# The low part of the attention query as a full 128-row tile

## The chip, the cores and the metric

One core of a Trainium2 chip runs the kernel. The metric is device microseconds (us) of one execution; lower is better. A change of about 0.5% is the least that a measurement of this kernel can tell from no change.

The core has five engines with a queue each: TensorE (PE in the profile; its weight loads are listed apart as PEld), VectorE (DVE), ScalarE (ACT), GpSimd (POOL) and SyncE (SP, which here issues the DMAs). A matrix product on TensorE is two instructions: a weight load of a stationary tile (here up to 128 rows by 128 columns) and a matmul that streams the columns of a moving tile through it. The rows are the partitions over which the product sums.

## The reference

The program is a stack of layers over 512 tokens of width 1024 (and 256 context tokens in the first ones): a recurrent mixer with a scan, then three attention layers. The change is in the attention layers alone. What they compute, cut to what matters:

```python
def block(q_blk):                                     # second layer: differential attention
    s = einsum("bqhcd,bkhcd->bchqk", q_blk, k_all) * scale      # 8 heads x 2 maps of 64 features
    p = softmax(s, axis=-1)
    attn = p[:, 0] - lam * p[:, 1]
    return einsum("bhqk,bkhe->bqhe", attn, v_all)               # 512 queries, 768 keys
...
s = einsum('bhqd,bhkd->bhqk', q, k) * dh ** -0.5      # third and fourth layer: 16 heads of 64 features,
p = softmax(where(mask, s, -inf), axis=-1)            # causal, dilated and memory heads, 512 queries
o = einsum('bhqk,bhkd->bhqd', p, v)
```

All inputs and outputs are float32.

## The kernel before

The first half of the program (`scan`, L935) is the recurrent mixer; it ends at about 1125 us of the execution. `dense` (L1788) does the rest: an output projection with a norm (`out_layer`, L1176), the differential attention (`phase_4`, L1480), an output projection, and twice an attention layer (`phase_5`, L1639) with an output projection behind it.

**Precision.** A float32 operand is split in two parts of the type fp32r, hi + lo = x, and a product is made of hi·hi, hi·lo and lo·hi. Projections do this in three matmuls (`mm3`, L1065; the matmul is at L1070). The scores q·k do it in two, since a head has only 64 features and the array has 128 rows: `split_k` (L1315) stores the keys of an even head as [hi; lo] over the 128 partitions and those of an odd head as [lo; hi]. `split_q` (L1322) stores the queries as [hi; hi] in a tile `q_hi` (L1326 and L1327, ScalarE) and their low part once in a tile `q_lo` (L1328, VectorE): even heads on partitions 0 to 63, odd heads on 64 to 127. `qk_tiles` (L1309) makes these tiles for two pairs of heads, two buffers each: `q_hi` is [128, 4, 512], `q_lo` is [128, 2, 512].

`scores` (L1362) then issues, for one head, one block of 128 queries and up to 512 keys, two products into the same PSUM columns:

```python
P.matmul(ps, q[0][:, 2 * j + h, c], k[h][:, j, a:a + n], start=True, stop=False)   # L1366, 128 rows
P.matmul(ps, q[1][r, j, c], k[h][r, j, a:a + n], start=False, stop=stop)           # L1367, 64 rows
```

The first sums q_hi·(k_hi + k_lo) over 128 rows, the second q_lo·k_hi over the 64 rows `r` of the head.

**Order of the work.** Each attention layer has four steps, one for each two pairs of heads. In a step, `attention` makes eight blocks, each in three pieces: a (scores, maximum, exponential, normalisation), b (transposes of the probabilities, L1566 or L1736) and c (the product with the values, L1577 or L1750). `pipeline` (L1395) runs a two blocks ahead of b and c. In between, `run_streams` (L1074) emits pieces of `side`: the gates of this step and the projections of the keys, queries and values of the next one (`heads`, L1254, `values`, L1299), which are L1070 products. The last step of a layer has only the gates and loads of the output projection beside it. `qk_tiles` of a step is called in the side stream of the step before (`kqv`, L1503; `qkv`, L1664), for the first step ahead of it (`mem`, L1654). The final order on each engine is set by a planner (L1917, `schedule_with_timeline_sim=True`) that works on its own estimates.

Of the other engines' work in a block: VectorE takes the maximum (L1542, L1705), ScalarE the exponential (L1546, L1713, L1717) and a scaling (L1555, L1724), GpSimd the difference of the two maps (L1556) or the scaling of one head (L1726). GpSimd also multiplies with the rope tables (L1293) and splits some of the weights (L1051).

Two other tiles share the names `q_lo` and `q_hi` and so their buffers: the residual of the context (L1796) and that of x (`resid`, L1391). A product over the transposed probabilities at L1750 uses 128 rows by 64 columns of the array, and the transposes and the products with values at L1566, L1577, L1736 all 128 by 128.

Of the kernel before, what the change touches and what calls it, by code (L numbers as in the profile page):

```python
# [8 lines left out]
FT = mybir.dt.float32  # L9
# [57 lines left out]
def rsqrt_dve(E, pool, v, n):  # L67
    """1 / sqrt(v) by Newton steps from a guess out of v's bits."""
    nc = E.nc
    y = pool.tile([128, n], FT, name="rq_y", bufs=2)  # L70
    t = pool.tile([128, n], FT, name="rq_t", bufs=2)
    nc.vector.tensor_scalar(y.bitcast(I32), v.bitcast(I32), -0.5, float(0x5F3759DF), OP.mult, OP.add)
    for _ in range(4):
        nc.vector.tensor_tensor(t, y, y, OP.mult)
        nc.vector.scalar_tensor_tensor(t, t, -0.5, v, OP.mult, OP.mult)
        nc.vector.scalar_tensor_tensor(y, t, 1.5, y, OP.add, OP.mult)
    return y


def ada_columns(E, pool, pp, w, n):  # L80
    """silu(c) @ w for the columns w(kb) = [128, 128 n] of each block kb, as [128, n, 2] in PSUM"""
    nc = E.nc
    ps = pp()
    for kb in range(8):
        nc.tensor.matmul(ps[0:2, 0:128 * n], E.cs[:, kb, :], w(kb), start=(kb == 0), stop=(kb == 7))
    row = pool.tile([2, 128 * n], FT, name="ada_r", bufs=1)
    nc.scalar.copy(row, ps[0:2, 0:128 * n])
    ps = pp()[:, 0:2 * n].rearrange("p (m c) -> p m c", c=2)
    for m in range(n):
        nc.tensor.transpose(ps[:, m, :], row[:, m * 128:(m + 1) * 128], E.ident[0:2, 0:2])  # L90
    return ps


def ada_bias(E, l, m0, n, ps):
    """columns m0 to m0 + n of the modulation of layer l out of those of silu(c) @ ada_w[l]"""
    E.nc.vector.tensor_tensor(E.mod[l][:, m0:m0 + n, :], ps, E.adab[:, l, m0:m0 + n].unsqueeze(2).to_broadcast([128, n, 2]),
                              OP.add)
# [8 lines left out]
def startup(E, hh, hl):  # L106
    """hh, hl: the first layer's normed and modulated [x of the context, x], transposed and split."""
# [59 lines left out]
class Blocks:  # L167
    """[128, 8, 128] of weights at a time in the order of their use, loaded and split ahead of it."""
# [37 lines left out]
class Scan:  # L206
    """The first mixer: its projections, the scan over both directions and its readout, eight pairs of heads in turn.
    Everything of a pair of heads has the heads in the halves of the partitions."""
# [9 lines left out]
    # the projections  # L218
# [10 lines left out]
    def project(self, rhs, evict, last=False):  # L229
        """evict(ps, a, n) for the columns a to a + n of the next block's rows over the tokens; last: uses the second  # L230
        part of the tokens ahead of all else"""
        E = self.E
        ws = self.W.get()
        ps = [self.pj() for _ in rhs]
        n = [0] * len(rhs)
        passes = [(half, part) for part in (((1,), (0, 2)) if last else ((0, 1, 2),)) for half in range(2)]
        for half, part in passes:
            wh, wl = ws[half]
            for gi, (hh, hl, a) in enumerate(rhs):
                terms = [((wh, hh), (wh, hl), (wl, hh))[i] for i in part]  # L240
                for kb in range(4 * half, 4 * half + 4):
                    for w, h in terms:
                        n[gi] += 1
                        E.nc.tensor.matmul(ps[gi][:, :256], w[:, kb % 4, :], h[:, kb, :], start=(n[gi] == 1),  # L244
                                           stop=(n[gi] == 24))
                if n[gi] == 24:
                    evict(ps[gi][:, :256], a, 256)
                yield 0
            if 0 in part:
                self.W.ahead(half)  # L250

    def head_rsqrt(self, x, n, scale, eps, use):
        """use(ps, a, n): ps the broadcast rsqrt(scale * sum of x^2 over each head + eps) of columns a to a + n"""
# [100 lines left out]
    def memory(self):  # L354
        """the memory's keys (normed, transposed) and values of both layers"""
# [41 lines left out]
    def memory_norm(self):  # L397
        """the memory, normed and transposed, to E.MT"""
# [19 lines left out]
    def ada(self, pieces, pool, psum, bufs=2):  # L418
        """more columns of the modulation: the first layer's gates and the second layer's columns"""
# [11 lines left out]
    # the scan  # L431
# [68 lines left out]
    def prep(self, p, g, j, d):  # L500
        """one direction of one head pair over one group of four chunks"""
# [5 lines left out]
        q = d * 64  # L507
# [85 lines left out]
    def fetch(self, k, jds):  # L593
        """the matrices of four chunks that were made ahead of the scan"""
# [23 lines left out]
    def invert(self, b):  # L618
        """the inverses of the unit lower triangular matrices of two groups, in place of their transposes"""
# [59 lines left out]
    def chain(self, a, js):  # L679
        """the scan over the chunks of the given blocks of every pair"""  # L680
# [209 lines left out]
    # the order of it all  # L890

    def weave(self, streams, until=lambda: False):
        """streams: [time of the next piece, order, generator, time from piece to piece, condition, boost]"""
# [41 lines left out]
def scan(E, stack):  # L935
    """the scan; returns the next layers' object with the first of its weights and of the scan's output already on chip"""
# [89 lines left out]
class Weights:  # L1026
    """The dense weights, [128, 8, 256] at a time, in the order of their use: loaded and split ahead of it."""
# [37 lines left out]
def mm3(E, ps, lh, ll, rh, rl, kbs=range(8), k=0):  # L1065
    """ps = sum over the 8 blocks of (lh + ll)^T (rh + rl), each a function of the block; k of the 24 products are in
    ps already."""
# [6 lines left out]
def run_streams(tc, main, side, n_main, n_side):  # L1074
    """Emits side's pieces in proportion between main's."""
# [15 lines left out]
class Dense:  # L1091
    """The layers after the scan: output projection of the first mixer, then the three attention layers."""
# [34 lines left out]
    def load_y(self, src, f0, f1, n, g0=0, ys=None):  # L1127
        """the features f0 to f1 of the groups g0 to n of 256 columns of src [8, 128, ..] in DRAM"""
# [13 lines left out]
    def tokens(self, ps, gs, tb, w, kbs=range(8), k=0):  # L1142
        """ps[128 tokens, n] of token block tb: gs hold 256 tokens each"""
# [5 lines left out]
    def features(self, ps, gs, w, c0):  # L1149
        """ps[128 features, 512] of the columns c0 to c0 + 128 of w"""  # L1150
# [5 lines left out]
    def gate_rows(self, g, n, gt):  # L1156
        """gt = columns n * 256.. of the gate g = (layer, kind) over all partitions"""
# [9 lines left out]
    def begin(self, kbs):  # L1167
        """the first blocks of the first output layer, as far as the features kbs go"""
# [7 lines left out]
    def out_layer(self, ys, resid, gate, norm, out=None, late=()):  # L1176
        """resid[tb] += gate * (y @ w); the next layer's norm follows block by block. late: the features that come
        last; the first blocks sum up the others ahead of them, each in a bank of its own."""
# [65 lines left out]
    def silu(self, ps, s):  # L1244
        """silu(ps) * 2 * s for a column or number s"""
# [8 lines left out]
    def heads(self, gs, tbs, w, tab, put):  # L1254
        """[128 tokens, 4 heads of 64]: rms norm, gain and rope (tab(i) gives their tables for block i, the second None
        without rope), then put(xs, i) transposes the blocks i and i + 1."""
# [52 lines left out]
    def qk_tiles(self, nk):  # L1309
        """Two pairs of heads, in two parts each, hi + lo = x. q: [hi; hi] of each head, and lo with the even heads on  # L1310
        the upper half; k: the even heads as [hi; lo], the odd ones as [lo; hi]."""
        q = self.pool.tile([128, 4, 512], FR, name="q_hi", bufs=2), self.pool.tile([128, 2, 512], FR, name="q_lo", bufs=2)
        return q, [self.pool.tile([128, 2, nk], FR, name="k_s", bufs=4) for _ in range(2)]

    def split_k(self, dst, src):  # L1315
        """both heads of src: dst gives the place in the tiles of the even and the odd one"""
# [5 lines left out]
    def split_q(self, hi, lo, src):  # L1322
        """both heads of src: hi [128, pairs, 2, n]"""
        V, A = self.E.nc.vector, self.E.nc.scalar
        for h, own, other in ((0, slice(0, 64), slice(64, 128)), (1, slice(64, 128), slice(0, 64))):
            A.copy(hi[own, :, h], src[own])  # L1326
            A.copy(hi[other, :, h], src[own])  # L1327
            V.tensor_tensor(lo[own], src[own], hi[own, :, h], OP.subtract)  # L1328

    def turned(self, xs, i, hs):  # L1330
        """the pairs hs of the blocks i and i + 1, [128, len(hs), 256]"""
# [13 lines left out]
    def turn_q(self, q):  # L1345
        def put(xs, i):
            c = slice(i * 128, i * 128 + 256)
            self.split_q(q[0].rearrange("p (j h) t -> p j h t", h=2)[:, :, :, c], q[1][:, :, c],
                         self.turned(xs, i, (0, 1)))
# [3 lines left out]
    def turn_qk(self, q, k, j):  # L1353
        def put(xs, i):
            c = slice(i * 128, i * 128 + 256)
            src = self.turned(xs, i, (0, 1))
            self.split_q(q[0].rearrange("p (j h) t -> p j h t", h=2)[:, j:j + 1, :, c], q[1][:, j:j + 1, c], src[:, 0:1])
# [4 lines left out]
    def scores(self, ps, q, k, j, h, qb, a, n, stop=True):  # L1362
        """ps = q k^T of the head h of the pair j for the query block qb and the keys a to a + n"""
        P, c = self.E.nc.tensor, slice(qb * 128, (qb + 1) * 128)
        r = slice(h * 64, h * 64 + 64)
        P.matmul(ps, q[0][:, 2 * j + h, c], k[h][:, j, a:a + n], start=True, stop=False)  # L1366
        P.matmul(ps, q[1][r, j, c], k[h][r, j, a:a + n], start=False, stop=stop)  # L1367
# [4 lines left out]
    def gated(self, y, f, t, c, ps, sg, last):  # L1372
        """the columns c of the feature block f of y, kept on chip in last or else in DRAM"""
# [21 lines left out]
    def pipeline(self, steps):  # L1395
        """steps: (a, b, c) of each block; a runs two blocks ahead."""
# [13 lines left out]
class Norm:  # L1410
    """rms norm of x's blocks, scaled by the columns g (and shifted by b), transposed and split into groups."""
# [54 lines left out]
def rope_tables(D, src, gains, nj):  # L1466
    """tables [128, 4, nj, 64] of cos * gain and sin * (swapped gain)"""
# [12 lines left out]
def phase_4(D, hg, Y):  # L1480
    """differential attention; hg: groups of the context and of the two halves of x"""
# [439 lines left out]
```

## Time and profile of the kernel before

| what | us |
|---|---|
| median of 3 runs | 2424.89 |
| the runs | 2416.70 to 2430.13 |
| span of the profiled execution | 2427.3 |
| TensorE busy in it | 2202.6 (91%) |
| TensorE's weight loads busy | 1902.4 (78%) |
| VectorE busy | 1560.4 (64%) |
| ScalarE busy | 1177.2 (48%) |
| GpSimd busy | 666.1 (27%) |

The page gives the profiled execution's time as its span, 2427.3 us, which lies within the three runs and 0.1% above their median. A matmul's row in the trace has its start and a modelled duration; matmuls are pipelined, so the next one starts before the row ends. What a matmul costs is therefore read from its start to the next start, not from its duration. In the timeline, like instructions that overlap are merged in one row with their count. The attention of the second layer fills about 1264 to 1672 us, that of the third 1777 to 2031 and of the fourth 2120 to 2376. The granted TensorE clock is given as a share: 1.0 is 2.4 GHz and 0.5 is 1.2 GHz.

### The profile page before, as it was taken

How to read it: one execution, taken by the hardware profiler on the slowest of the kernel's cores; microseconds unless marked ns; L12 is line 12 of the kernel's file. 1: busy time of each engine (PE TensorE's matmuls, PEld its weight loads, DVE VectorE, ACT ScalarE, POOL GpSimd, SP SyncE). 2: the span in 40 equal slices, each digit the busy share in tenths (PEclk: the TensorE clock that was granted, in tenths of full speed). 3: DMA queues.
4: the chain of work that ended last, by engine and by line, in shares of the span. 5: the costliest groups of instructions: out<-in, count | busy, mean ns of one | idle time of the engine just before them, and what ended most of it. 6: DMA issues, size and time to landing. Idle time of an engine off the chain costs nothing. (4 is left out here: it accounts for less than half of the span.)

```text
span 2427.3 us, 50739 instructions
## 1 busy us (share of the span) xinstructions
PE 2202.6 (91%) x19736; PEld 1902.4 (78%) x19736; DVE 1560.4 (64%) x3937; ACT 1177.2 (48%) x2676; POOL 666.1 (27%) x969
## 2 busy tenths in 40 slices
PE   6999999986889998876989999998899999999999
PEld 3998899875767676655978888876887887987888
DVE  5477889694478686524675676754676574766563
ACT  4456465662353544322445455463455554555562
POOL 0133436242136264212212222221222222022221
PEclk9999999997998678887999999997899999999999
DMA  7466464448444233334211111120322122311122
GB/s 235 143 205 210 128 226 159 128 139 261 150 127 134 73 114 92 119 105 166 72 58 39 54 40 62 40 87 18 109 70 72 63 75 89 129 62 58 61 87 88
DMA packets 190720, 263.73 MB, mean 109 GB/s; under 512 B 16144, under 2 KB 137488, under 8 KB 190352
## 3 DMA queue, kind: packets, MB, share of 16 engines
q1 hardware_dynamic: 190480, 260.48, 33.6%
q8 instruction: 156, 2.56, 0.4%
q14 instruction: 84, 0.69, 0.1%
HBM read 197.24 MB, written 63.18 MB: 107 GB/s over the span
## 5 line engine op out<-in xcount | busy, mean ns | idle before, releaser
L1070 PE MATMUL ps_pj<-w_hi,act 128*128 128x256 f32 x3264 | 650.0, 294 | 16.0 <-ACT act L1450 3.8
L1070 PEld LDWEIGHTS ps_pj<-w_hi,act 128*128 128x128 f32 x3264 | 531.6, 197 | 31.5 <-ACT act L1450 5.5
L1070 PE MATMUL ps_pj<-w_lo,act 128*128 128x256 f32 x1632 | 475.0, 291 | 0.0
L244 PE MATMUL ps_pj<-h,b_hi 128*128 128x256 f32 x1760 | 334.4, 288 | 1.5 <-ACT gh L343 1.3
L1070 PEld LDWEIGHTS ps_pj<-w_lo,act 128*128 128x128 f32 x1632 | 321.5, 197 | 3.0 <-issue 0.5
L244 PEld LDWEIGHTS ps_pj<-h,b_hi 128*128 128x128 f32 x1760 | 276.2, 191 | 9.6 <-issue 4.5
L244 PE MATMUL ps_pj<-h,b_lo 128*128 128x256 f32 x880 | 250.1, 287 | 1.3 <-POOL b_lo L190 1.0
L244 PEld LDWEIGHTS ps_pj<-h,b_lo 128*128 128x128 f32 x880 | 168.0, 191 | 5.2 <-issue 2.5
L1726 POOL TENSOR_SCALAR p<-p,r 128x128 f32<-128x128 f32 (+2 forms) x64 | 74.2, 1159 | 278.3 <-DVE r L1720 207.3
L1070 PE MATMUL ps_pj<-act,w_hi 128*128 128x256 f32 x768 | 148.3, 287 | 0.0
L1049 ACT CAST w_hi<-w_raw 128x1024 fp32r<-128x1024 f32 x120 | 121.1, 1051 | 53.3 <-PE ps_pj L1070 21.5
L1051 POOL TENSOR_TENSOR w_lo<-w_raw,w_hi 128x1024 fp32r<-128x1024 f32 x30 | 72.4, 2414 | 260.1 <-ACT w_hi L1049 228.2
L1051 DVE TENSOR_TENSOR w_lo<-w_raw,w_hi 128x1024 fp32r<-128x1024 f32 x90 | 119.9, 1339 | 35.7 <-ACT w_hi L1049 35.2
L570 PE MATMUL ps_b<-al,bk 64*128 64x128 f32 x768 | 123.2, 303 | 13.7 <-DVE rbk L578 10.9
L570 PEld LDWEIGHTS ps_b<-al,bk 64*128 64x128 f32 x768 | 102.1, 202 | 30.4 <-issue 16.0
L1070 PEld LDWEIGHTS ps_pj<-act,w_hi 128*128 128x128 f32 x768 | 121.3, 191 | 1.5 <-issue 0.7
L1556 POOL TENSOR_TENSOR p<-p 128x768 f32<-128x768 f32 x32 | 60.9, 1904 | 195.8 <-ACT p L1555 129.2
L1367 PE MATMUL ps_s<-k_s,q_lo 64*128 64x256 f32 (+2 forms) x256 | 112.7, 443 | 0.0
L1366 PE MATMUL ps_s<-k_s,q_hi 128*128 128x256 f32 (+2 forms) x256 | 105.9, 416 | 7.4 <-ACT p L1546 4.0
L538 POOL TENSOR_TENSOR s<-bk,src 64x256 f32<-64x256 f32 x96 | 78.0, 812 | 121.9 <-DVE bk L535 108.6
L1070 PE MATMUL ps_pj<-act,w_lo 128*128 128x256 f32 x384 | 109.1, 284 | 0.0
L1293 POOL TENSOR_TENSOR hx<-hx,ctab 128x256 f32<-128x256 f32 x80 | 67.2, 856 | 133.0 <-DVE ht L1291 111.0
(322 smaller groups left out, 4911.0 us busy)
## 6 DMA issues: line engine op xcount, KB each, us to landing
w_raw<-in_wd_dram SPq DMA_DIRECT2D x120, 512.0 KB, 4.3
b_raw<-in_blocks_dram SPq DMA_DIRECT2D x84, 256.0 KB, 3.1
src<-streams SPq DMA_DIRECT2D x48, 384.0 KB, 3.9
ada_s<-in_ada_w_dram SPq DMA_DIRECT2D x32, 512.0 KB, 4.3
vs<-streams SPq DMA_DIRECT2D x48, 256.0 KB, 3.6
ada_w<-in_ada_w_dram SPq DMA_DIRECT2D x8, 1024.0 KB, 11.2
lr<-lora SPq DMA_DIRECT2D x96, 64.0 KB, 3.4
streams<-k SPq DMA_DIRECT2D x32, 192.0 KB, 2.9
```

Of the source, the lines that this page charges most:

```text
L244: E.nc.tensor.matmul(ps[gi][:, :256], w[:, kb % 4, :], h[:, kb, :], start=(n[gi] == 1), stop=(n[gi] == 24))
L538: G.tensor_tensor(v3(rev(s))[a:a + 64], ut[a:a + 64, 1 if a == 0 else 0], v3(rev(r))[a:a + 64], OP.mult)
L570: P.matmul(pb[:, c, :], bk[q:e, c].rearrange("p s t -> p (s t)"), al[q:e, c, h:3:2 - h, :], start=True, stop=True, tile_position=(q, 0))
L1049: nc.scalar.copy(hi[:, a:a + 4], raw)
L1051: e.tensor_tensor(lo[:, a:a + 4], raw, hi[:, a:a + 4], OP.subtract)
L1070: E.nc.tensor.matmul(ps, a(kb), b(kb), start=(k == 0), stop=(k == 23))
L1293: G.tensor_tensor(w4(x), w4(x), cb, OP.mult)
L1366: P.matmul(ps, q[0][:, 2 * j + h, c], k[h][:, j, a:a + n], start=True, stop=False)
L1367: P.matmul(ps, q[1][r, j, c], k[h][r, j, a:a + n], start=False, stop=stop)
L1556: G.tensor_tensor(ps_[0], ps_[0], ps_[1], OP.add)
L1726: G.tensor_scalar(t, t, r[:, h:h + 1], None, OP.mult)
```

## The change

`q_lo` becomes [128, 4, 512], as large as `q_hi`: each head has a place of its own, its low part on its own 64 partitions and zeros on the other 64. The zeros are written by two GpSimd memsets in every call of `qk_tiles`, each over 64 partitions and 2 x 512 numbers. `split_q` writes the low part to the new place. `scores` issues its second product with all 128 rows: the extra rows multiply the zeros with the other part of the key. The memory for the larger tile (2 buffers, 4 KB more of each partition for each) goes with a smaller scratch area for dynamic DMAs. The rest of the diff takes comments and docstrings out.

```diff
     def qk_tiles(self, nk):
-        q = self.pool.tile([128, 4, 512], FR, name="q_hi", bufs=2), self.pool.tile([128, 2, 512], FR, name="q_lo", bufs=2)
+        q = [self.pool.tile([128, 4, 512], FR, name=n, bufs=2) for n in ("q_hi", "q_lo")]
+        for h, other in ((0, slice(64, 128)), (1, slice(0, 64))):
+            self.E.nc.gpsimd.memset(q[1].rearrange("p (j h) t -> p j h t", h=2)[other, :, h].bitcast(FT), 0.0)
         return q, [self.pool.tile([128, 2, nk], FR, name="k_s", bufs=4) for _ in range(2)]
...
             A.copy(hi[own, :, h], src[own])
             A.copy(hi[other, :, h], src[own])
-            V.tensor_tensor(lo[own], src[own], hi[own, :, h], OP.subtract)
+            V.tensor_tensor(lo[own, :, h], src[own], hi[own, :, h], OP.subtract)
...
-            self.split_q(q[0].rearrange("p (j h) t -> p j h t", h=2)[:, :, :, c], q[1][:, :, c],
-                         self.turned(xs, i, (0, 1)))
+            self.split_q(*[t.rearrange("p (j h) t -> p j h t", h=2)[:, :, :, c] for t in q], self.turned(xs, i, (0, 1)))
...
-            self.split_q(q[0].rearrange("p (j h) t -> p j h t", h=2)[:, j:j + 1, :, c], q[1][:, j:j + 1, c], src[:, 0:1])
+            self.split_q(*[t.rearrange("p (j h) t -> p j h t", h=2)[:, j:j + 1, :, c] for t in q], src[:, 0:1])
...
-        r = slice(h * 64, h * 64 + 64)
-        P.matmul(ps, q[0][:, 2 * j + h, c], k[h][:, j, a:a + n], start=True, stop=False)
-        P.matmul(ps, q[1][r, j, c], k[h][r, j, a:a + n], start=False, stop=stop)
+        for i in range(2):
+            P.matmul(ps, q[i][:, 2 * j + h, c], k[h][:, j, a:a + n], start=(i == 0), stop=(stop and i == 1))
...
-    nc = bacc.Bacc("TRN2", target_bir_lowering=False, num_devices=1)
+    nc = bacc.Bacc("TRN2", target_bir_lowering=False, num_devices=1, dynamic_dma_scratch_size=1024)
```

## Rows read from the trace of the kernel before

**Rows 1.** Table by stage: stretch, us, busy PE, PEld, DVE, ACT, POOL (instructions), clock, DMA share, GB/s.

```profile
1264.00:1603.00 339.00, 328.15 (x2313) 290.42 (x2312) 216.28 (x539) 181.50 (x384) 83.01 (x58) 0.97 0.15 50
1603.00:1672.00 69.00, 58.85 (x266) 42.79 (x265) 40.49 (x104) 37.74 (x80) 16.90 (x9) 0.78 0.19 62
1777.00:1980.00 203.00, 194.83 (x1439) 168.54 (x1438) 135.37 (x355) 113.77 (x300) 55.46 (x50) 0.96 0.21 69
1980.00:2031.00 51.00, 47.96 (x340) 37.35 (x339) 32.85 (x96) 32.80 (x72) 14.09 (x11) 0.97 0.33 102
```

**Rows 2.** What PE waited for, 1264 to 2376 us: total, times, longest; first and last.

```profile
PE ps_t L1335 <- DVE hx L1294: 12.6, 6, 3.0
...
PE ps_s L1070 <- ACT p L1713: 0.3, 1, 0.3
```

**Rows 3.** PE's timeline around one block's score products: start, us, engine, line, operation.

```profile
1302.56 0.28 PE L1070 MATMUL ps_pj<-w_lo,act 128*128 128x256 f32 x1
1302.68 0.40 PE L1366 MATMUL ps_s<-k_s,q_hi 128*128 128x512 f32 x1
1303.01 0.50 PE L1367 MATMUL ps_s<-k_s,q_lo 64*128 64x512 f32 x1
1303.44 0.39 PE L1366 MATMUL ps_s<-k_s,q_hi 128*128 128x256 f32 x1
1303.76 0.38 PE L1367 MATMUL ps_s<-k_s,q_lo 64*128 64x256 f32 x1
1304.07 0.51 PE L1070 MATMUL ps_pj<-w_hi,act 128*128 128x256 f32 x2
1304.41 0.28 PE L1070 MATMUL ps_pj<-w_lo,act 128*128 128x256 f32 x1
```

**Rows 4.** The same view, where a 512-column L1366 stands among L1070 products.

```profile
1272.66 0.40 PE L1366 MATMUL ps_s<-k_s,q_hi 128*128 128x512 f32 x1
1272.89 0.28 PE L1070 MATMUL ps_pj<-w_lo,act 128*128 128x256 f32 x1
```

**Rows 5.** The same view, where two L1367 stand together: first and last of four places.

```profile
1779.88 0.28 PE L1070 MATMUL ps_pj<-w_hi,act 128*128 128x256 f32 x1
1780.08 0.49 PE L1367 MATMUL ps_s<-k_s,q_lo 64*128 64x256 f32 x2
1780.51 0.39 PE L1070 MATMUL ps_pj<-w_hi,act 128*128 128x256 f32 x1
1780.73 0.28 PE L1070 MATMUL ps_pj<-w_lo,act 128*128 128x256 f32 x1
...
2126.18 0.50 PE L1367 MATMUL ps_s<-k_s,q_lo 64*128 64x256 f32 x2
```

**Rows 6.** The instructions of L1367: duration in ns, min/median/max, first and last start.

```profile
L1367 PE MATMUL ps_s<-k_s,q_lo x256: 271/384/793, 1273.7 to 2372.0; 64*128 64x512 f32 x76, 64*128 64x256 f32 x40, 64*128 64x384 f32 x12
```

**Rows 7.** PE's timeline, L1750 beside L1367: first and last of 24 places.

```profile
1792.21 0.66 PE L1750 MATMUL ps_t<-pt,v 128*64 128x128 f32 x8
...
2364.44 0.55 PE L1750 MATMUL ps_t<-pt,v 128*64 128x128 f32 x6
```

**Rows 8.** PE's timeline at the lower clock: four score products between these two rows.

```profile
1640.22 0.77 PE L1366 MATMUL ps_s<-k_s,q_hi 128*128 128x512 f32 x1
...
1642.66 0.47 PE L1566 MATMUL ps_t<-ident,p 128*128 128x128 f32 x1
```

**Rows 9.** The table by stage for this block alone, columns as in rows 1.

```profile
1640.20:1642.70 2.50, 2.50 (x7) 1.18 (x6) 0.29 (x1) 1.25 (x4) 0.00 (x0) 0.50 0.00 0
```

**Rows 10.** Groups of POOL's memsets: busy us, mean ns, idle before and what ended it.

```profile
L635 POOL MEMSET ut<- 128x1024 f32 x6 | 5.7, 954 | 0.2
...
L695 POOL MEMSET xz<- 64x256 f32 x8 | 3.3, 416 | 65.5 <-DMA ada_s<-in_ada_w_dram 49.1 <-PE ps_o L782 15.5 <-DVE brk L817 0.7
```

**Rows 11.** DMA issues of the weights: queue, operation, count, size, median us to landing.

```profile
w_raw<-in_wd_dram SPq DMA_DIRECT2D x120, 512.0 KB, 4.3
```

**Rows 12.** The group of PE's weight loads of L1070: busy us, mean ns, idle before.

```profile
L1070 PEld LDWEIGHTS ps_pj<-w_hi,act 128*128 128x128 f32 x3264 | 531.6, 197 | 31.5 <-ACT act L1450 5.5
```

## The prediction

> **What bounds the kernel now.** I read the table by stage first, since a busy share over the whole span says nothing of the stage in question, then PE's waits, and last PE's timeline, product by product. In the table, while attention and projections run side by side, PE is busy for 328 of 339 us in the second layer and 195 of 203 us in the third, with VectorE next at 216 and 135 us; in each layer's last step, which has few projections, it is 59 of 69 and 48 of 51 us [rows 1]. The fourth layer repeats the third's two stretches. The list of what PE waited for has 21 entries over the 1112 us from 1264 to 2376, from 12.6 us down to 0.3 us [rows 2]; they add up to some 63 us, 6%. So PE sets the pace, and time taken out of PE's own stream comes off the end, except where a wait takes its place.
>
> PE's stream holds the time that the change is after. A 256-column product of 128 rows next to another costs 0.12 us from start to start (1302.56 to 1302.68) [rows 3]; a 512-column one among such products costs 0.23 us (1272.66 to 1272.89) [rows 4]. The four score products of one map of one block start at 1302.68, 1303.01, 1303.44 and 1303.76, the next projection at 1304.07, and two projections behind take until 1304.41 [rows 3]. That is 1.73 us for two 512-column and four 256-column products, which at the undisturbed prices cost 2 x 0.23 + 4 x 0.12 = 0.94 us. The excess, 0.79 us, lies around four borders between a 128-row and a 64-row product: 0.20 us a border, half before and half behind it.
>
> Is it the border or the 64-row product that costs? At four places two L1367 stand together. From the projection at 1779.88 to the second one behind them at 1780.73 it is 0.85 us for four 256-column products, 0.37 us above 0.48 [rows 5]. There are two borders and two 64-row products: 0.185 us for each border, none between the two. In the usual order each low product has two borders, and pays about 0.39 us. So the border costs, and I take 0.195 us for one, between the two readings.
>
> **What the change removes.** L1367 runs 256 times [rows 6], so there are 512 borders. The four places where two stand together have two fewer each (8). At 24 places an L1367 stands beside L1750 [rows 7], whose products use 128 rows by 64 columns: that is a border before, and with 128 by 128 in L1367's place it is one still. 512 - 8 - 24 = 480 borders go: 480 x 0.195 = 94 us. At the lower clock a border costs more: from 1640.22 to 1642.66 the four score products take 2.44 us [rows 8], at a granted clock of 0.50, which is 1.2 GHz [rows 9]. Streaming at half the pace would take 2 x (0.46 + 0.24) = 1.40 us, and the 1.04 us above it lie on three and a half borders: 0.30 us each. By the clock column about 10% of the attention time ran there (3% of 339 us, 22% of 69 us, 4% and 3% of the later stretches, each counted twice since the clock halves) [rows 1]; 48 borders x 0.1 us add 5 us. Gross: 99 us.
>
> **What it adds and moves.** The second product streams the same columns over 128 rows instead of 64. No row shows a duration that depends on the rows, and the 128-row L1366 at 0.23 us for 512 columns [rows 4] is the product that L1367 turns into; bounds 0 and 0, since the same instruction is in the trace.
>
> Two memsets in each call of `qk_tiles`, four calls in each of three layers: 24 on GpSimd, each 64 partitions by 1024 numbers. A memset of 128 by 1024 takes 0.954 us, one of 64 by 256 0.416 us in the mean [rows 10]; four of these would be 1.7 us. Nearest is the first, with the same count per partition: 24 x 0.95 = 23 us of GpSimd, which is busy for only a quarter of these stretches [rows 1]. They are emitted a whole step ahead of the first score that reads the tile, so I cost them at nothing. The cover is the lead of two blocks that the scores have; without it L1556 or L1726, queued behind the memsets, would hand its probabilities to PE late, up to 23 us (by the smaller memset's rate 40 us) in all. The new wait, of the memset for the last readers of the buffer, falls on GpSimd; of that more below.
>
> `split_q` keeps its instructions (L1326 to L1328): only the place written differs, 0. The smaller scratch touches DMAs alone. All DMA issues in the list are SP's; a weight tile lands in 4.3 us [rows 11] while PE has at least 96 products of the tile before, 11.5 us, so the landing could double and stay covered: 0. The planner may order PE's queue otherwise; third and fourth layer, planned apart, take 254 and 256 us, so I count 0, with 2 us a layer either way.
>
> **What comes back.** In the last step of each layer PE already waits for the softmax (10 of 69 us idle in the second layer, 3 of 51 in the others) [rows 1]. These stretches have 32, 16 and 16 low products, so 64 + 30 + 30 = 124 of the borders (two beside L1750 in each of the later layers), 24 us and 3 us for the low clock. All of the 27 us could come back as longer waits, or none; there is idle time on PE but also PE-bound work between, so I take half, 13 us. In the other stretches 72 us go. VectorE would then be busy for 216 of about 300 us (72%) and 135 of 186 us (73%): not a new bound, but queues in order wait a little more; between 0 and 20 us (a third more than the 63 us of today) I take 8.
>
> Sum: 99 - 13 - 8 = 78 us. From the span of 2427.3 that is 2349; the span is 2.4 us above the median, so against the median I predict **2347 us**.
>
> **A rule against it.** PE's full-row products follow at 0.12 us with a weight load for each, although a weight load takes 0.197 us in the mean [rows 3, 12]: the loads overlap the streaming before them. The Trainium skill, page "TensorE: Matmul & The Clock Gate", Part 3, has it that a weight load overlaps a running matmul only when the two use different row groups. By that rule two full-row products would always expose the load, the second score product would cost as much after the change as now, and the sum would be 0 instead of 78 us. The spacing of L1070 speaks against it.
>
> **Rivals.** (1) *The softmax chain takes over.* Once PE is a tenth faster in attention, VectorE's maxima, the exponentials and GpSimd's pass set the pace for good. For it: in the second layer's last step PE is idle for 15%. Against: the 6% of waits, and two blocks of lead. All 27 us and 20 us come back, and the memsets take half of 23 us: 99 - 58 = 41 us, about 2384.
>
> (2) *Nothing changes*, because a weight load is exposed behind any product of the same rows and the 0.2 us are its price. Then L1367 with 128 rows costs what it costs: 2425 us. Against it stand L1070 and the lone L1366 [rows 3, 4].
>
> (3) *Slower: a memset stands in GpSimd's queue.* A memset waits until the last scores that read its buffer are through, and what is queued behind it on GpSimd, L1556 or L1726 of the running step, waits too; PE then lacks the transposes. That such a wait can be long, a memset of before shows: one group has 65.5 us of idle time ahead of it, 49.1 us for a DMA [rows 10]. It decides from 99 / 12 = 8 us of lost PE time per call of `qk_tiles`. If the planner sets the pair one block too early, PE loses about a block, 108 us for eight in the second layer, 13.5 us: 12 x 13.5 - 99 = 63 us slower, 2488 us. Against it: the buffer was last read in the step before the running one, whose scores are all issued when the memset is emitted.
>
> **How the numbers follow.** The forecast has 0.80, rival 1 0.11, rival 2 0.03, rival 3 0.03, and 0.03 is left for an order of the planner that moves more than all this, either way. About 0.5% (12 us) is what a measurement of this kernel can tell from no change. Faster by more: the forecast, rival 1 and a part of the rest, 0.93; within 0.5%: rival 2 and some of the rest, 0.04; slower: rival 3, 0.03. Low end: all 99 us, and 15 us from the clock: some 89 us of attention ran at half clock [rows 1], where a product takes up to twice its time, so a full rise would give up to 44 us, and a third of it 15: 2425 - 114 = 2311. High end: rival 1, 2385.
>
> **What would show it.** Right: no 64-row product in the scores; the four score products and the two projections behind them 0.9 to 1.0 us apart in all instead of 1.73; the attention stretches 25 to 40 us shorter in the second layer and 18 to 25 in the third and fourth; the first 1264 us and the output projections as they are; PE's waits up from 63 to 75 to 95 us. Wrong: score products that still start 0.3 and 0.4 us apart (rival 2); shorter products but PE's waits up by over 50 us, for VectorE and ScalarE (rival 1); idle PE before L1566 or L1736 with GpSimd held by a memset (rival 3); or a clock column well below 0.95 in the stretches of before.

## The result and the profile after

The changed kernel takes **2353.53 us** (median of 4 runs, 2343.63 to 2356.17) where the kernel before takes 2424.1 us (4 runs, 2416.7 to 2430.13): a ratio of 0.969 [0.9655, 0.9724]. A second set of the changed kernel on another chip gave 2351.26 us against 2422.13, 0.9694 [0.9661, 0.9727]. The prediction was 2347 us, in a range of 2311 to 2385.

First PE's timeline in the changed kernel, around one block's score products in the second layer. Both score products are issued at L1367 there; columns as in [rows 3].

```profile
1303.38 0.28 PE L1070 MATMUL ps_pj<-w_lo,act 128*128 128x256 f32 x1
1303.50 0.40 PE L1367 MATMUL ps_s<-k_s,q_hi 128*128 128x512 f32 x1
1303.74 0.40 PE L1367 MATMUL ps_s<-k_s,q_lo 128*128 128x512 f32 x1
1303.97 0.28 PE L1367 MATMUL ps_s<-k_s,q_hi 128*128 128x256 f32 x1
1304.09 0.28 PE L1367 MATMUL ps_s<-k_s,q_lo 128*128 128x256 f32 x1
1304.21 0.41 PE L1070 MATMUL ps_pj<-w_hi,act 128*128 128x256 f32 x2
1304.45 0.28 PE L1070 MATMUL ps_pj<-w_lo,act 128*128 128x256 f32 x1
```

Here 512 columns take 0.23 to 0.24 us to the next start and 256 columns 0.12. From the first score product to the third projection behind them it is 0.95 us, where it was 1.73 us [rows 3].

Next the table by stage (columns as in [rows 1]), cut from the first to the last score product of each layer. The kernel before, second, third and fourth layer:

```profile
1272.70:1666.40 393.70, 372.72 (x2459) 319.30 (x2458) 248.06 (x625) 211.67 (x447) 94.84 (x62) 0.94 0.15 50
1777.80:2026.90 249.10, 238.76 (x1747) 202.92 (x1746) 164.88 (x440) 143.96 (x365) 67.75 (x60) 0.96 0.22 73
2120.00:2372.00 252.00, 241.23 (x1764) 205.01 (x1762) 165.42 (x442) 144.26 (x367) 67.34 (x60) 0.96 0.22 71
```

The changed kernel, the same three, and then the last step of the second, third and fourth layer, the first two to be held against the 69 us and the 51 us of [rows 1]:

```profile
1271.90:1619.60 347.70, 317.44 (x2459) 305.07 (x2458) 248.25 (x624) 209.68 (x444) 98.68 (x67) 0.97 0.17 56
1729.50:1962.60 233.10, 219.12 (x1747) 197.41 (x1746) 164.59 (x438) 142.44 (x364) 72.17 (x65) 0.96 0.23 78
2057.40:2294.10 236.70, 221.33 (x1763) 198.97 (x1762) 165.87 (x444) 143.39 (x367) 70.14 (x63) 0.97 0.22 75
...
1565.00:1623.00 58.00, 41.60 (x264) 36.43 (x263) 39.52 (x103) 37.24 (x79) 16.29 (x10) 0.88 0.20 68
...
1917.00:1966.00 49.00, 43.83 (x347) 36.26 (x347) 36.08 (x96) 32.69 (x73) 17.75 (x15) 1.00 0.36 120
2247.80:2298.30 50.50, 42.58 (x329) 33.89 (x328) 34.38 (x93) 32.45 (x72) 12.82 (x11) 1.00 0.30 99
```

The fourth layer's last step in the kernel before:

```profile
2326.00:2376.00 50.00, 46.97 (x330) 36.30 (x330) 31.84 (x92) 32.73 (x72) 14.03 (x11) 0.97 0.31 99
```

The three layers give 46.0, 16.0 and 15.3 us, together 77.3 of the 77.6 us by which the spans differ (2427.3 and 2349.7). The rest of the program stands: the first score product starts at 1271.9 us instead of 1272.7, VectorE and ScalarE do the work they did, and GpSimd does 11 us more in the three stretches, the memsets' work. In the last steps PE's idle time goes from 10 to 16 us, from 3 to 5 us and, in the fourth layer, from 3 to 8 us; that last step is no shorter than it was.

Then the list of what PE waited for, changed kernel, 1262 to 2298 us (total, times, longest), its head and its end:

```profile
PE ps_t L1589 <- DVE o L1586: 13.6, 5, 4.4
PE ps_t L1337 <- DVE hx L1287: 6.4, 2, 4.0
PE ps_t L1566 <- POOL p L1556: 6.0, 4, 2.5
PE ps_s L1367 <- ACT p L1546: 5.5, 3, 2.9
PE ps_s L1367 <- ACT p L1717: 5.5, 10, 0.9
PE ps_t L1736 <- POOL p L1726: 5.4, 10, 1.9
...
PE ps_s L1070 <- ACT p L1713: 0.3, 1, 0.3
```

Its 27 entries add up to 82 us, against 63 us in 21 entries before. The new waits are spread over the softmax chain: for ScalarE, which has not yet read the score buffer (L1546, L1717), and for GpSimd's pass over the probabilities (L1556, 1.6 us before, and L1726, 0.5 us before). No entry names a memset. Last, the group of the memsets among GpSimd's groups over that stretch:

```profile
L1314 POOL MEMSET q_lo<- 64x1024 f32 x20 | 19.0, 949 | 1.3 <-PE ps_s L1367 0.2
```

One takes 0.949 us, and GpSimd was idle for only 1.3 us before all 20 of them together, 0.2 us of it for the last readers of the buffer.

### The profile page after: what moved, and what is told of

It is laid out like the page before. It is cut to its first block, busy times and chain, and to the rows that moved or that the text cites. A ratio compares the mean times of both kernels' runs of the same rounds, so it can differ in the third digit from the quotient of the medians.

```text
span 2349.7 us, 50767 instructions
## 1 busy us (share of the span) xinstructions
PE 2110.8 (90%) x19736; PEld 1879.3 (80%) x19736; DVE 1563.5 (67%) x3937; ACT 1174.7 (50%) x2676; POOL 687.4 (29%) x993
## 5 line engine op out<-in xcount | busy, mean ns | idle before, releaser
L1070 PE MATMUL ps_pj<-w_hi,act 128*128 128x256 f32 x3264 | 646.5, 292 | 20.4 <-ACT act L1450 5.2
L1070 PEld LDWEIGHTS ps_pj<-w_hi,act 128*128 128x128 f32 x3264 | 530.4, 196 | 34.3 <-ACT act L1450 7.3
L1070 PE MATMUL ps_pj<-w_lo,act 128*128 128x256 f32 x1632 | 471.2, 289 | 0.0
L1070 PEld LDWEIGHTS ps_pj<-w_lo,act 128*128 128x128 f32 x1632 | 319.7, 196 | 0.6 <-issue 0.2
L1070 PE MATMUL ps_pj<-act,w_hi 128*128 128x256 f32 x768 | 146.2, 286 | 0.0
L1726 POOL TENSOR_SCALAR p<-p,r 128x128 f32<-128x128 f32 (+2 forms) x64 | 71.9, 1123 | 237.2 <-DVE r L1720 144.5
L1070 PEld LDWEIGHTS ps_pj<-act,w_hi 128*128 128x128 f32 x768 | 120.9, 191 | 0.4 <-issue 0.2
L1070 PE MATMUL ps_pj<-act,w_lo 128*128 128x256 f32 x384 | 109.6, 285 | 0.0
L1556 POOL TENSOR_TENSOR p<-p 128x768 f32<-128x768 f32 x32 | 60.6, 1894 | 158.8 <-ACT p L1555 100.1
L1367 PE MATMUL ps_s<-k_s,q_hi 128*128 128x256 f32 (+2 forms) x256 | 91.2, 365 | 14.7 <-ACT p L1546 5.5
L85 PE MATMUL ps_m<-ada_s,cs 128*2 128x128 f32 x512 | 76.8, 313 | 19.7 <-DMA ada_s<-in_ada_w_dram 17.0
```

What stands on the lines that cost most here:

```text
L1070: E.nc.tensor.matmul(ps, a(kb), b(kb), start=(k == 0), stop=(k == 23))
L1367: P.matmul(ps, q[i][:, 2 * j + h, c], k[h][:, j, a:a + n], start=(i == 0), stop=(stop and i == 1))
L1556: G.tensor_tensor(ps_[0], ps_[0], ps_[1], OP.add)
L1726: G.tensor_scalar(t, t, r[:, h:h + 1], None, OP.mult)
```

## The experiments

The theory: the time comes from the borders between 128-row and 64-row products, and from nothing else in the change. The rivals on trial: the layout, memsets or scratch do it (or cost something that a part of the gain hides), and the half-row product itself is dear. The edits are made on the changed kernel or on the kernel before, as said. The first four below shared a chip (2424.35 us for the kernel before); the zeros written once, the remaining borders and the first run of the grouped order another (2424.57 us); the 96 rows and the last two runs a third (2422.13 us).

**Everything but the rows** (changed kernel; the low product back on its 64 rows, with the new layout, memsets and scratch kept):

```diff
-        for i in range(2):
-            P.matmul(ps, q[i][:, 2 * j + h, c], k[h][:, j, a:a + n], start=(i == 0), stop=(stop and i == 1))
+        r = slice(h * 64, h * 64 + 64)
+        P.matmul(ps, q[0][:, 2 * j + h, c], k[h][:, j, a:a + n], start=True, stop=False)
+        P.matmul(ps, q[1][r, 2 * j + h, c], k[h][r, j, a:a + n], start=False, stop=stop)
```

> The changed kernel with one thing undone: the low product reads 64 rows again, from the new padded tile; memsets, larger tile, small scratch and the planner's new order stay. Border theory (the time is paid where TensorE goes from 128 rows to 64 and back): the 480 borders are back, the memsets are hidden, so 2425 us within 8 us. Memset theory (GpSimd's memsets hold up the softmax, and the changed kernel gained in spite of them): 2432 to 2448 us, with new waits of PE for GpSimd.

Measured: 2421.4 us (10 runs), ratio 0.9987 [0.996, 1.0014]. Its timeline around a block's score products (L1367 is the first product here, L1368 the second), and its second layer in the table by stage:

```profile
1303.47 0.40 PE L1367 MATMUL ps_s<-k_s,q_hi 128*128 128x512 f32 x1
1303.80 0.50 PE L1368 MATMUL ps_s<-k_s,q_lo 64*128 64x512 f32 x1
1304.22 0.39 PE L1367 MATMUL ps_s<-k_s,q_hi 128*128 128x256 f32 x1
1304.54 0.38 PE L1368 MATMUL ps_s<-k_s,q_lo 64*128 64x256 f32 x1
1304.85 0.51 PE L1070 MATMUL ps_pj<-w_hi,act 128*128 128x256 f32 x2
```

```profile
1264.90:1652.60 387.70, 367.05 (x2460) 314.60 (x2458) 247.19 (x625) 211.46 (x447) 100.93 (x68) 0.96 0.15 50
```

The spacing of 0.3 and 0.4 us is back, and with it the time. Padding, 24 memsets and scratch together are worth nothing that can be measured; the rows of the second product are the whole gain.

**Scratch alone** (kernel before):

```diff
-    nc = bacc.Bacc("TRN2", target_bir_lowering=False, num_devices=1)
+    nc = bacc.Bacc("TRN2", target_bir_lowering=False, num_devices=1, dynamic_dma_scratch_size=1024)
```

> The kernel before with the small scratch for dynamic DMAs alone. Border theory and every other that I hold: no difference, 2425 us within 5 us, since all DMAs are issued by SP. If the scratch took part in these DMAs: slower, with longer landings.

Measured: 2424.88 us (10 runs), 0.9979 [0.9957, 1.0002]. No difference.

**Fewer borders with the half-row product kept** (kernel before; all first products of a block, then all second ones, in both attentions; the one in `phase_5` is shown):

```diff
-            for h in range(2):
-                w = max(n, 256)
-                D.scores(ps[:, h, :w], q, k, j % 2, h, qb, 0, w, j >= 6)
+            w = max(n, 256)
+            for part in range(2):
+                for h in range(2):
+                    D.scores(ps[:, h, :w], q, k, j % 2, h, qb, 0, w, j >= 6, part)
...
+        if part == 0:
+            P.matmul(ps, q[0][:, 2 * j + h, c], k[h][:, j, a:a + n], start=True, stop=False)
+        else:
+            P.matmul(ps, q[1][r, j, c], k[h][r, j, a:a + n], start=False, stop=stop)
```

> The kernel before with another order alone: of each block, all 128-row score products come first and then all 64-row ones. Rows, tiles and the number of products stay. The program's order has 255 borders that the change would remove instead of 480. Border theory: 225 borders x 0.195 = 44 us less on PE, a fifth of it given back as waits, so about 2390 us (2380 to 2400). Rival (each 64-row product, or each weight load behind a product of the same rows, costs its 0.39 us in any order): 2425 us within 5 us. If even and odd heads' products overlapped once they stand together: below 2380 us.

Measured: 2389.82 us (4 runs), 0.9829 [0.9796, 0.9862]: 34.5 us less by the medians, 41 by the ratio. Every product is the one of before, only the order differs. Counted over the order of PE's products in the trace, the low products have 282 neighbours of another number of rows or columns instead of 504, so 222 borders fewer.

What a border costs is read in the second layer, where no two products run side by side. There the score products and the product right behind each group of them, each to the next start less PE's idle time, take 84.0 us; with the old order they take 111.0 us (kernel before), 109.4 (everything but the rows) and 108.4 (scratch alone). With 126 borders fewer that is 0.19 to 0.21 us a border. In the changed kernel they take 62.7 us, with 256 borders fewer: 0.18 to 0.19 us. The two nearly agree, so the price is one of the border and not of the half-row product.

In the third and fourth layer the same reading gives 28.5 us for 96 borders, 0.30 us each. There the new order also lets 50 pairs of low products run side by side (last section), so the run saves time of two kinds, and that it came out at the 2390 us expected from borders alone is in part luck. A place with one border pair for two low products (in this kernel L1369 is the low product):

```profile
1311.48 0.51 PE L1367 MATMUL ps_s<-k_s,q_hi 128*128 128x512 f32 x2
1311.92 0.62 PE L1369 MATMUL ps_s<-k_s,q_lo 64*128 64x512 f32 x2
1312.47 0.50 PE L1070 MATMUL ps_pj<-w_hi,act 128*128 128x256 f32 x2
1312.81 0.28 PE L1070 MATMUL ps_pj<-w_lo,act 128*128 128x256 f32 x1
```

From 1311.48 to 1312.81 it is 1.33 us for two 512-column and four 256-column products, 0.39 us above the undisturbed 0.94: two borders, where [rows 3] paid for four.

**Full rows in the second layer only** (changed kernel):

```diff
+        r = slice(0, 128) if full else slice(h * 64, h * 64 + 64)
...
-                D.scores(ps[:, h, :w], q, k, j % 2, h, qb, 0, w, j >= 6)
+                D.scores(ps[:, h, :w], q, k, j % 2, h, qb, 0, w, j >= 6, False)
```

> The changed kernel with 128-row low products in the second layer (differential attention) alone; third and fourth layer use 64 rows. Additive theory: the second layer's 46 us come off the end whole and the 31 us of the later layers do not, so about 2380 us (2374 to 2386). Rival (what the second layer gains is partly given back where the third layer starts): 2385 to 2400 us.

Measured: 2373.58 us (4 runs), 0.9793 [0.9747, 0.984]. Its three stretches:

```profile
1266.60:1614.00 347.40, 315.58 (x2460) 303.13 (x2458) 248.33 (x624) 209.34 (x445) 99.00 (x67) 0.98 0.17 56
1723.90:1971.30 247.40, 236.10 (x1745) 201.09 (x1745) 166.20 (x440) 143.32 (x365) 71.69 (x66) 0.97 0.22 74
2067.70:2316.00 248.30, 239.08 (x1746) 202.58 (x1746) 166.31 (x440) 143.36 (x365) 69.81 (x64) 0.96 0.21 72
```

The second layer is as in the changed kernel, the others as in the one with everything but the rows (247.9 and 248.7 us). The gains add up by layer: some 50 us in the second and some 20 in the other two by the medians. The time is 6 us below the expected 2380, just under the range; with an interval of 11 us to either side this does not show that the second layer holds more of the gain than was thought.

**Zeros written once** (changed kernel; two padded tiles are kept through the program, with 4 memsets in place of 24):

```diff
+        if self.nq < 2:
+            z = self.pool.tile([128, 4, 512], FR, name="q_lo", bufs=2)
...
+            self.zq.append(z)
+        q.append(self.zq[self.nq % 2])
```

> The changed kernel with the zeros written once: two padded tiles are kept for all three layers, 4 memsets instead of 24. Border theory with hidden memsets: 2353 us within 6 us. Memset theory: 5 to 23 us faster, 2330 to 2348 us.

Measured: 2356.33 us (4 runs), 0.9729 [0.9692, 0.9766]: no faster than the changed kernel. The memsets are hidden.

**96 rows instead of 128** for the low product of even heads (changed kernel), to ask whether the zeros must fill the array:

```diff
+        r = slice(0, 128 if h else 96)
...
+        P.matmul(ps, q[1][r, 2 * j + h, c], k[h][r, j, a:a + n], start=False, stop=stop)
```

> The changed kernel with 96 rows instead of 128 in the low product of the even heads (rows 96 to 127 hold zeros, so nothing is lost); odd heads keep 128. Half of the low products have a row count of their own again. Theory A (a border is a change between the full array and a tile of it of 64 rows or fewer; 96 rows still take the full array): as the changed kernel, 2353 us within 6 us, products 0.12 and 0.23 us apart. Theory B (every change of the row count drains): 240 of the borders are back, 47 us on PE, so about 2391 us (2383 to 2400).

Measured: 2347.87 us (4 runs), 0.9693 [0.9659, 0.9727]. PE's timeline around an even head's score products, the second one at L1368:

```profile
1304.08 0.40 PE L1367 MATMUL ps_s<-k_s,q_hi 128*128 128x512 f32 x1
1304.31 0.39 PE L1368 MATMUL ps_s<-k_s,q_lo 96*128 96x512 f32 x1
1304.54 0.28 PE L1367 MATMUL ps_s<-k_s,q_hi 128*128 128x256 f32 x1
1304.66 0.29 PE L1368 MATMUL ps_s<-k_s,q_lo 96*128 96x256 f32 x1
1304.79 0.29 PE L1070 MATMUL ps_pj<-w_lo,act 128*128 128x256 f32 x1
```

The spacings are 0.23, 0.23, 0.12 and 0.13 us: 96 rows next to 128 cost no border, 64 rows next to 128 do. Over the three layers the score products and the product behind each group of them take 120.4 us here and 120.6 us in the changed kernel.

**The remaining borders** (changed kernel). L1750, the product with the values in the third and fourth layer, uses 128 rows by 64 columns. Here one product of 128 rows by 128 columns serves both heads, over 256 moving columns, and VectorE picks the useful halves with one more multiplication:

```diff
-                for h in range(2):
-                    o = (j % 2) * 128 + h * 64
-                    P.matmul(ps[h * 64:h * 64 + 64, :128], v[:, kb, o:o + 64], pt[:, h, kb, :], start=(kb == 0),
-                             stop=(kb == nk - 1), tile_position=(0, h * 64))
+                P.matmul(ps[:, :256], v[:, kb, o:o + 128], pt[:, :, kb, :], start=(kb == 0), stop=(kb == nk - 1))
...
+            V.tensor_tensor(O[j][0:64, c], ps[0:64, 0:128], SG[j][0:64, c], OP.mult)
```

> The changed kernel, and in the third and fourth layer the product with the values as one 128 x 128 product over both heads' 256 columns, of which half is used, in place of two products of 128 rows by 64 columns. Takes away the 182 borders to 128 x 64 that were left in the changed kernel's trace; adds one small VectorE multiplication for each of 64 blocks. Border theory holding for columns as for rows: 182 x 0.19 = 35 us less, 304 wider products at some 0.05 us more each (15 us), and a quarter given back: about 15 us faster, 2338 us (2325 to 2350). Rival (a change of the columns drains nothing, and the wider product only costs): 2365 to 2375 us.

Measured: 2349.66 us (4 runs), 0.9696 [0.9658, 0.9734]; a **miss**: at the far end of what was expected, and not to be told from the changed kernel. Its third and fourth layer:

```profile
1727.60:1962.80 235.20, 216.59 (x1614) 200.53 (x1614) 177.31 (x467) 142.70 (x364) 71.80 (x65) 0.99 0.24 78
2057.90:2293.00 235.10, 217.20 (x1615) 201.97 (x1615) 177.23 (x467) 142.93 (x364) 69.94 (x63) 0.99 0.23 76
```

They are as long as in the changed kernel. In the trace no two neighbours on PE differ in shape any more in these stretches. Summing each product's time to the next product's start, less PE's idle time, the score products of the third layer fall from 24.6 to 21.4 us, and what is neither score nor value product by 5 us, in part by the clock (0.99 against 0.96). But the values rise from 23.5 us (264 products, 0.178 us for a pair) to 29.0 us (132, 0.22 us each), and PE's idle time rises from 14.0 to 18.6 us, with VectorE busy for 13 us more. A border of that kind was cheaper than the columns and the VectorE work that buy it off.

**Grouped order on top of the change**, to see what the order is worth without borders (the order of the third experiment, both products with 128 rows), and then the changed kernel and this one once more on one chip:

> The changed kernel (128 rows in both products) with the order of the grouped run: all high products of a block first, then all low ones. Control for the grouped run. Border theory: there is no border left to save, so the order alone is worth nothing, 2353 us within 6 us. Rival (the order itself, by earlier or later maxima, made the grouped run's difference): as far from 2353 us as the grouped run is from 2425 us.

> The changed kernel once more, beside the next one on the same chip: 2353 us within 6 us.

> The changed kernel with all high products of a block ahead of all low ones, once more, beside the changed kernel on the same chip. Its first run had a median 12 us below the changed kernel's, with overlapping intervals, where the border theory has no reason for a difference. Border theory: 2353 us within 6 us, no difference from the run beside it. Rival (the order is worth something in the third and fourth layer, whose stretches were 3 and 8 us shorter in the first run's profile): 8 to 12 us faster than the run beside it.

Measured: 2341.91 us (4 runs), 0.9664 [0.9621, 0.9707]. On the third chip 2343.33 us (6 runs), 0.9674 [0.9642, 0.9706], beside 2351.26 us for the changed kernel, 0.9694 [0.9661, 0.9727]. The third and fourth layer of the changed kernel and then of the grouped one, both from that chip:

```profile
1734.70:1968.00 233.30, 217.78 (x1746) 196.63 (x1746) 164.89 (x439) 142.20 (x364) 71.57 (x65) 0.97 0.24 78
2064.70:2297.40 232.70, 217.11 (x1762) 195.29 (x1762) 165.79 (x445) 143.06 (x367) 70.09 (x63) 0.99 0.23 77
```

```profile
1735.30:1965.40 230.10, 217.49 (x1746) 196.52 (x1746) 163.76 (x439) 141.95 (x364) 72.25 (x65) 0.97 0.24 79
2060.90:2288.50 227.60, 215.91 (x1761) 195.25 (x1762) 164.02 (x445) 143.33 (x367) 70.75 (x63) 0.99 0.23 77
```

PE is busy as long within 1 us, and the stretches are 3 and 5 us shorter, mostly in idle time. The second layer goes the other way: 354.3 us grouped beside 350.3, as in the first pair of profiles (352.5 beside 347.7), each time at a clock lower by 0.01 or 0.02. The medians stand 8 us apart on this chip, and the first pair, on two chips, 12 us in the same direction, but the intervals overlap. That grouping helps a little is likely and not settled.

## Why the prediction was right, and which terms were not

**The border is the cost.** Right. Undoing the rows alone gives the whole time back, removing 222 borders with the half-row product in place gives about half of it (a part through the pairs side by side), and 479 borders are gone against 480 forecast.

The weight loads, which the prediction read beside L1070 alone, show what a border is. PEld's rows at the place of [rows 3], before, and then around the products shown above, changed:

```profile
1302.57 0.19 PEld L1366 LDWEIGHTS ps_s<-k_s,q_hi 128*128 128x128 f32 x1
1303.01 0.18 PEld L1367 LDWEIGHTS ps_s<-k_s,q_lo 64*128 64x128 f32 x1 [0.25 <-issue]
1303.44 0.19 PEld L1366 LDWEIGHTS ps_s<-k_s,q_hi 128*128 128x128 f32 x1 [0.24 <-issue]
```

```profile
1303.51 0.19 PEld L1367 LDWEIGHTS ps_s<-k_s,q_lo 128*128 128x128 f32 x1
1303.74 0.19 PEld L1367 LDWEIGHTS ps_s<-k_s,q_hi 128*128 128x128 f32 x1
```

Between like products the load starts when the product before has just begun and runs under it: at 1302.57 for the product of 1302.68, at 1303.51 for that of 1303.74. At a border it starts only with its own product, at 1303.01 and 1303.44, and PEld is idle before it. In the trace of the kernel before this holds at all 244 steps from 128 to 64 rows, while in the run with 96 rows a load for 96 rows behind 128 leads its product by 0.12 us, as between like ones. So a border is a place where the weight load does not run ahead. How its 0.2 us divides between this load and a wait for the product before is not shown.

The Trainium skill, page "TensorEngine Tiling (Array Packing)", Key Properties, states: changing the tiling mode, and not just the tile, drains TensorE. The traces agree in that 64 rows against 128 cost time at each change; for 96 against 128 they show no cost.

**Its price was set a little too high.** Both readings, 0.195 and 0.185 us, came from places where PE had nothing else to wait for. A border's time falls half on the product before it and half on the one behind. So the score products and the product behind each group of them are added up over the three stretches, each to the next start less idle time: they fall from 208.3 us (second to fourth layer 111.0, 48.6 and 48.6) to 120.6 us (62.7, 29.5 and 28.4). That is 87.6 us, or 0.18 us for each of 479 borders, where the sum had 94 + 5. All else loses 7 us between these two profiles, and under 1 us between the two of like clock that follow. The granted clock was 0.94 in the second layer of before and 0.97 after, while the kernel with everything but the rows had 0.96 there and a stretch of 387.7 us, 6 us less than before with the same borders. Held against that kernel, the second run of the changed one (350.3 us at 0.95) gives 37 us in the second layer, and 15 and 16 us in the others: 68 us net. With the growth of the waits put back (41.4 to 59.9 us) that is 86 us gross, where 99 was forecast.

The cheapest borders lead into the causal mask's products (L1701 and L1703, in bf16), 38 of the 480. Between the same two kernels a projection of 256 columns behind a low product falls from 0.22 to 0.12 us in the median, but a mask product of 128 columns takes 0.066 us behind either, and one of 256 columns 0.12: half of such a border costs nothing. The 5 us added for the low clock could not be told apart.

**What came back** was 21 us in the forecast and is 17 to 18 us. PE's idle time grows from 42.1 to 59.6 us over the three stretches (21.0, 10.3, 10.8 to 30.3, 14.0, 15.4). For the last steps 13 us were foreseen, half of the 27 us at stake, and 6, 2 and 5 us came, 13 in all; half was a guess, and the layers did not share it alike: the fourth layer's last step gave everything back. The other stretches lost the remaining 4 or 5 us, with 8 foreseen. The whole list of waits, 82 us, lies in the forecast 75 to 95. So a gross term some 13 us too large met a return some 3 us too large, and that the errors went against each other is luck: the medians moved by 71 us (75 by the ratio) where 78 was the forecast, and the two profiles by 77.6 us with some help from the clock.

**By layer the prediction missed**: 25 to 40 us in the second and 18 to 25 in the third and fourth were asked for, 46, 16 and 15 came. These bounds did not follow from its own terms. The second layer has 256 of the borders, at 0.195 us 50 us, which less half of the waits puts about 40 in the middle of a range and not at its end. The others have 107 and 116, 21 and 23 us, which is 17 and 18 with the 4 and 5 us by which their idle time grew taken off. At like clock, 37, 15 and 16 us come near to that.

**Costs set at nothing** were nothing: memsets at 0.949 us each (0.95 forecast) show in no wait of PE, and writing 4 in place of 24 gains nothing; the scratch gives 0.9979 [0.9957, 1.0002]; the 128-row low product streams like the first one.

**The rivals fell.** The softmax chain did not take over: VectorE is busy for 216 of 301 us in the first three steps of the second layer, 72%, as forecast, and PE's waits rose by 19 us, not by 50. "Nothing changes" fell with the timeline: four 128-row products in a row, each with a weight load of its own, start 0.23 and 0.12 us apart. That rival had half of it right: the 0.2 us do go with a load that does not run ahead, but only where the shape changes, not behind every product of the same rows. By the Trainium skill, page "TensorE: Matmul & The Clock Gate", Part 3, a weight load overlaps a running matmul only when the row groups differ; the trace of this case disagrees, with loads of all 128 rows that run under products of all 128 rows. And no memset held GpSimd's queue. The clock rose little with the change, if at all: the granted clock of the second layer's stretch was 0.94 and 0.96 with the old borders and 0.94 to 0.98 without any, that of the fourth 0.96 and 0.97 with them and 0.97 to 0.99 without. No run shows the 15 us that the low end of the range had for it.

## What to carry to other kernels

When a matmul that uses half the rows of the array stands between full ones, read the start-to-start time on both sides of it and compare it with two full neighbours: here each change between 128 and 64 rows cost 0.18 to 0.2 us, more than the whole 256-column product (0.12 us), and zeros in the unused rows cost nothing. If the padding is not to be had, put the odd-shaped products next to one another, which brought about half of it with no change to the data. But price what the padding adds, since the product with the values showed the limit: more streamed columns and one more VectorE pass ate what its borders gave back.

## What was not expected of the hardware

Two 64-row products for different halves of the array can run side by side. In the grouped kernel (low product at L1369), where an even head's (partitions 0 to 63) and an odd head's (64 to 127) stand together in the third and fourth layer, PE's timeline has:

```profile
1848.18 0.40 PE L1367 MATMUL ps_s<-k_s,q_hi 128*128 128x256 f32 x2
1848.52 0.39 PE L1369 MATMUL ps_s<-k_s,q_lo 64*128 64x256 f32 x2
1848.83 0.43 PE L1754 MATMUL ps_t<-pt,v 128*64 128x128 f32 x2
```

The two of L1369 cover 0.39 us together, as long as a single one takes in the experiment with everything but the rows (0.38 us at 1304.54); in the records their starts are 3 ns apart. Of the 52 pairs of neighbouring low products in these two layers 50 start together like this. The 63 pairs of the second layer, where both are of the same half, do not, nor do the pairs of [rows 5] (0.49 us); why the latter do not is not shown. By the 0.30 us for a border in these layers against 0.19 to 0.21 in the second, the pairs saved about 10 us in all (an estimate). Padding still pays more here: a pair takes 0.31 us to the next start, borders in it, where two 256-column products of 128 rows take 0.24 us. Nor was it foreseen that 96 rows next to 128 are free.
